# TensorE put into a written order in a two-block transformer kernel, with the first weights of a stage taken four at a time, weight splits held back at the norms and the attention heads handled in pairs

## The chip, the cores and the metric

One core of one Trainium2 chip runs the kernel. The metric is the device time of one execution in microseconds (us); the kernel before took 1275.31 us, the median of 3 runs (1269.11 to 1276.87 us).

## What is computed

256 positions of width 1024 go through two blocks of two layers each, in fp32. Cut to the lines that matter, the first block is

```python
for i in range(DEPTH):                      # 2
    hn = rmsnorm(h, norm_mix[i])
    mix = diff_attention(hn, ...) if i % 2 == 0 else neighborhood_attention(hn, ...)
    h = h + mix
    h = h + swiglu(rmsnorm(h, norm_ffn[i]), ffn_w_gate[i], ffn_w_up[i], ffn_w_down[i])
    gate = jax.nn.sigmoid(rmsnorm(h, norm_ple[i]) @ ple_w_gate[i])
    h = h + gate * (p[i] @ ple_w_proj[i])
```

and the second block is

```python
for layer in range(DEPTH):
    hn = rmsnorm_2(h, mix_norm_g[layer])
    h = h + (even_mixer(hn, ...) if layer % 2 == 0 else odd_mixer(hn, ...))
    h = h + conv_ffn(rmsnorm_2(h, ffn_norm_g[layer]), ...)
return rmsnorm_2(h, final_norm_g)
```

The differential attention ("da") has 8 heads with two 64-wide maps each, the neighbourhood attention ("na") 16 heads of 64, the odd mixer ("od") 8 forgetting and 8 T5-biased causal heads of 64. The hidden width of each of the four FFNs is 2816.

## The kernel before, in words

Activations lie with features on the 128 partitions and the 256 positions along the free axis. An fp32 product is made of three fp32r matmuls of a high and a low part (`mm3`, L207): hi·hi, hi·lo, lo·hi. One output tile of a 1024-deep product is 8 x 3 = 24 matmuls, a `pair` of output tiles (L329) 48.

Weights (L51 to L103) come in chunks of 128 x 1024: SyncE loads a chunk into one of 5 stage buffers, ScalarE writes its high part `w_hi` (L88), VectorE the low part `w_lo` (L89), into one of 8 pairs of buffers. `take` (L97) hands out the next finished chunk, and each call first splits the chunk that is six ahead.

Each stage ends in a norm. While the last down projections of a stage run bank by bank (`Acc.last`, L355), VectorE adds a bank to the residual `h`, and ScalarE and VectorE write the next stage's input `u_hi`, `u_lo` and its squares. `rstd_a` (L278) sums the squares on TensorE (`ps_ss`), VectorE scales (L287), GpSimd raises to the power -1/2 (L288); `rstd_b` spreads the result over the partitions by two transposes on TensorE (`ps_r`, L304) and a ScalarE copy `R` (L306). The products of the next stage start before `R` is there, since it is multiplied in after them.

Work that hangs on earlier results is put off with `at(delay, f)` (L214) and done by `tick()` (L218), which is called after every 12 matmuls. `rstd_soon` (L312) puts `rstd_a` one tick and `rstd_b` three ticks after the end of a stage. In attention the table LAG (L34) holds the delays of scores, transposes, values. One differential head lists 12 score matmuls (3 for each of two maps and two query halves). The other two kinds list the scores head by head: 6 fp32r matmuls for an na head; for an od head one fp32 product 128 wide and 3 fp32r matmuls. The two heads of a pair use partitions 0 to 63 and 64 to 127 of the same tiles.

The order on all engines is chosen by the scheduler of the language. It starts from the order in which the code is written, and may move an instruction past others on its engine.

The lines of the steps: FFN L733 (`silu_times` L722), gate ("ple") L779, even mixer ("ev") with its list of eight pairs L909, `small_constants` with 8 bias tiles of the differential attention on VectorE L507 to L511, `pair_steps` L588, the end `finish` L940.

Of the kernel before, what the change touches and what calls it, by code (L numbers as in the profile page):

```python
# [33 lines left out]
LAG = {"da": (2, 8, 11, 14), "da_every": 3, "pair": (2, 5, 7), "every": 2}  # L34
# [18 lines left out]
class Weights:  # L53
# [4 lines left out]
    def __init__(self, nc, stage, split, chunks):  # L58
        self.nc, self.stage, self.pool, self.chunks = nc, stage, split, chunks
        self.loaded, self.done, self.taken = [], [], 0  # L60
        self.n_load = self.n_split = 0

# [44 lines left out]
def network(ctx: ExitStack, tc: tile.TileContext, x_t, p_t, cols, b_v, na_bias, t5_bias, w_mats, out):  # L107
    nc = tc.nc

# [28 lines left out]
    def add_ffn(gu, down):  # L138
        for j in range(FT):
            add(gu, 2 * j, 2 * j + 1)  # L140
            if j >= 2 and j % 2 == 0:
                if j < FT - 2:
                    add(down, j - 2, j - 1)
        add(down, FT - 4, FT - 3, FT - 2, FT - 1)
# [167 lines left out]
    def rstd_soon(n, a=1, b=3):  # L312
# [16 lines left out]
    def pair(u, tag="g", bufs=2):  # L329
        ps = psum.tile([128, 2, S], F32, tag=tag, bufs=bufs, name="ps_g")  # L330
        for i in range(2):
            out_tile(ps[:, i, :], u)
        return ps

    class Acc:
# [19 lines left out]
        def last(self, xs, k0, done):  # L355
            ws = [W.take(1024) for _ in xs]
# [22 lines left out]
    def transposes(a, skip):  # L379

        w = 384 if skip else 512
        ps = psum.tile([128, 512], F32, tag=att_tag["T"][0], bufs=att_tag["T"][1], name="ps_t")
# [40 lines left out]
    def qkv_group(n, g, kind, bv, steps):  # L423
# [12 lines left out]
        ps = pair(u)  # L436
# [9 lines left out]
        ps = pair(u)  # L446
# [47 lines left out]
    def score(o, q, k, r, p, qt, w):  # L494
        c = slice(qt * 128, (qt + 1) * 128)
        if w < S:
            mm(o, q[0][r, p, c], k[0][r, p, :w], True, True)
        else:
            mm3(o, (q[1][r, p, c], q[2][r, p, c]), (k[1][r, p, :], k[2][r, p, :]), True, True)
# [31 lines left out]
    def da_steps(g, q, k, v, bias, o, emitted):  # L531
        for p in range(2):
# [3 lines left out]
            def scores(p=p, hd=hd, box=box):  # L536
                ps = [att_psum("S").rearrange("p (a b) -> p a b", a=2) for _ in range(2)]
                for qt in range(2):
                    for m in range(2):
                        score(ps[m][:, qt, :], q, k, slice(64 * m, 64 * m + 64), p, qt, S)  # L540
# [42 lines left out]

            for delay, f in zip(LAG["da"], (scores, trans, values, back)):
                at(LAG["da_every"] * p + delay, f)


    def pair_steps(g, q, k, v, bias_of, is_causal, o, emitted, later):  # L588
        for p in range(2):
            box = {}  # L590
            for e in range(2):
                hd = 4 * g + 2 * p + e
                r = slice(64 * e, 64 * e + 64)

                def scores(p=p, e=e, hd=hd, r=r, box=box):
                    widths = (128, 256) if is_causal else (256, 256)
                    bias = bias_of(hd)
                    ps = att_psum("S").rearrange("p (a b) -> p a b", a=2)
                    for qt in range(2):
                        score(ps[:, qt, :widths[qt]], q, k, r, p, qt, widths[qt])  # L600
                    sc = work.tile([128, 2, S], F32, tag="sc", bufs=3, name="sc")
                    st = softmax_pair(sc, ps, bias, widths)
# [5 lines left out]
                def trans(e=e, box=box):  # L608
                    box["t", e] = transposes(box["s", e], is_causal)

                every = LAG["every"]
                at(later + every * (2 * p + e) + LAG["pair"][0], scores)
                at(later + every * (2 * p + e) + LAG["pair"][1], trans)
# [13 lines left out]
            at(later + every * (2 * p + 1) + LAG["pair"][2], values)  # L627

    def attention(n, kind, gain_next):
# [4 lines left out]
        for g in range(4):  # L634
            bv = None
            if kind == "na":
# [3 lines left out]
                bias_of = lambda hd, bt=bt: (bt[:, hd % 4, 0, :], bt[:, hd % 4, 1, :])  # L640
            elif kind == "od" and g < 2:
                bias_of = lambda hd: fox_bias(hd, extra)
            elif kind == "od":
                bias_of = lambda hd: (t5_tiles[0][:, hd - 8, 128:], t5_tiles[0][:, hd - 8, :])
# [3 lines left out]
            def steps(q, k, v, g=g):  # L648
                if kind == "da":
                    da_steps(g, q, k, v, da_tiles, o, emitted)  # L650
                else:
                    pair_steps(g, q, k, v, bias_of, kind == "od", o, emitted, 5 if kind == "od" and g == 0 else 0)
# [38 lines left out]
    def fox_prepare(z, extra):  # L691
# [18 lines left out]
        cum()  # L710

    def fox_bias(hd, extra):
        ps = att_psum("V")
        for t in range(2):
            nc.tensor.transpose(ps[:, t * 128:(t + 1) * 128], extra["f"][:, t, hd:hd + 1].to_broadcast([128, 128]), ident)
        b = work.tile([128, 384], F32, tag="fb", bufs=2, name="fb")
        for qt, (a, w) in enumerate(((0, 128), (128, 256))):
            nc.vector.scalar_tensor_tensor(b[:, a:a + w], causal[:, S - w:], extra["f"][:, qt, hd:hd + 1],
                                           ps[:, :w], op0=OP.add, op1=OP.subtract)
        return b[:, :128], b[:, 128:]  # L720
# [12 lines left out]
    def ffn(n, middle, gain_next, finish=None):  # L733
        acc = Acc(FT)
        mids = {}
        for j in range(FT):
# [7 lines left out]
        for j in range(FT - 4, FT - N_LAST):  # L744
            acc.step(mids.pop(j), j)
# [33 lines left out]
    def ple(n, l, gain_next, after, final=False):  # L779
        nn = Norm()  # L780
        pt = [t.rearrange("p (k s) -> p k s", k=2) for t in p_split[l]]
        for b in range(4):
            hi, lo = W.take(512)
            pp = psum.tile([128, 2, S], F32, tag="m", bufs=2, name="ps_p")
# [4 lines left out]
            pg = pair(n.u)  # L789
            z = work.tile([128, 2, S], F32, tag="a", bufs=3, name="z")  # L790
            nc.vector.tensor_mul(z, pg, bc2(n.R))
            t = work.tile([128, 2, S], F32, tag="sc", bufs=3, name="tz")
            nc.scalar.activation(t, z, AF.Tanh, scale=0.5)
            nc.vector.scalar_tensor_tensor(t, t, 1.0, pp, op0=OP.add, op1=OP.mult)
            hb = h[:, 2 * b:2 * b + 2, :]
            nc.vector.scalar_tensor_tensor(hb, t, 0.5, hb, op0=OP.mult, op1=OP.add)
            norm_bank(nn, b, hb, gain_next)
            stats_bank(nn, b, hb)
            if final:
                stats_bank(nn, b, hb, True)  # L800
# [109 lines left out]
    for i, (f, a) in enumerate(plan):  # L910
        ps = pair(n.u, tags[i], 2 if tags[i] == "g" else 1)
# [27 lines left out]

    def finish():  # L940
# [3 lines left out]
        def done(b, ps):  # L944
# [4 lines left out]
            if b % 2 == 0:  # L949
                po.append([psum.tile([128, 512], F32, tag="g", bufs=2, name="po") for _ in range(2)] if b == 0 else  # L950
                          [psum.tile([128, 512], F32, tag=f"acc{t}", name="po") for t in range(2)])
            for i in range(2):
                k = 2 * b + i
                for t in range(2):
# [150 lines left out]
```

## Time and profile before

| what | value |
|---|---|
| median of 3 runs | 1275.31 us |
| the profiled execution | 1277.65 us, span 1275.8 us |
| PE (TensorE) busy | 1253.6 us, 98% |
| DVE (VectorE) busy | 932.6 us, 73% |
| ACT (ScalarE) busy | 697.3 us, 55% |
| POOL (GpSimd) busy | 31.6 us, 2% |
| mean granted TensorE clock | 0.996 |

The span is what the trace covers; 1.85 us of the execution lie around it. Busy time of PE is modelled, and matmuls overlap each other there, so what one matmul costs is read from the distance of its start to the next one's start, here called its slot. The stages lie in the span like this: loads to about 7 us, da attention to 134, FFN to 318, ple to 355, na attention to 476, FFN to 662, ple to 695, ev to 778, conv FFN to 953, od attention to 1080, conv FFN to 1266.

### The profile page before, as it was taken

What the parts mean: (1) busy time and instruction counts of PE and PEld (TensorE: products, weight loads), DVE (VectorE), ACT (ScalarE), POOL (GpSimd) and SP (SyncE); (2) the same over time, 40 slices, a digit from 0 to 9 for tenths busy, and PEclk for the clock granted to TensorE, in tenths of its full rate; (3) what the DMA queues carried; (4) which work ended last, traced back from release to release, by engine and by line L of the source; (5) the groups of instructions that cost most, each with busy time, mean ns of one, the idle gap of its engine ahead of it and who ended that gap; (6) DMA issues with size and microseconds to landing.
All of it is one profiled execution on the core that took longest, in us unless ns stands there. A gap on an engine that the chain in (4) does not pass through costs nothing.

```text
span 1275.8 us, 25715 instructions
## 1 busy us (share of the span) xinstructions
PE 1253.6 (98%) x10448; PEld 1223.2 (96%) x10448; DVE 932.6 (73%) x1708; ACT 697.3 (55%) x1178; POOL 31.6 (2%) x56
## 2 busy tenths in 40 slices
PE   6999999999999999999999999999999999999997
PEld 6999999999989999999999999999999899999997
DVE  7886866666976667666678888777787766877774
ACT  6776644444666654444457456455456565544543
POOL 1011000000010000000000000000000000000000
PEclk9999999999999999999999999999999999999999
DMA  8465555554646536555546375555545333655530
GB/s 292 150 195 184 167 184 194 192 184 150 212 152 186 175 116 199 187 197 186 176 141 207 132 247 183 183 185 196 182 153 197 102 132 131 209 188 183 188 127 34
DMA packets 62935, 222.46 MB, mean 174 GB/s; under 512 B 7264, under 2 KB 7776, under 8 KB 62688
## 3 DMA queue, kind: packets, MB, share of 16 engines
q1 hardware_dynamic: 60768, 214.52, 49.8%
q0 software_dynamic: 1616, 5.77, 1.9%
q8 instruction: 82, 1.34, 0.4%
q10 hardware_dynamic: 432, 0.53, 0.1%
q14 instruction: 37, 0.30, 0.1%
HBM read 219.74 MB, written 1.05 MB: 173 GB/s over the span
## 4 chain that ended last, share of the span: by engine, by line
PE 88%; DVE 4%; issue 3%; ACT 2%; POOL 1%; DMA 1%; POOLq 0%; DVEq 0%; ACTq 0%; SPq 0%
PE ps_g L202 50%; PE acc L202 25%; PE ps_v L202 5%; PE ps_S L202 3%; PE ps_V L202 2%; DVE w_lo L89 2%; PE ps_t L388 1%; ACT w_hi L88 1%; POOL rstd L288 1%; ACT u_hi L263 1%; PE ps_p L202 1%; PE pz L202 0%; PE ps_ss L202 0%; DVE u_lo L265 0%; DVE h L366 0%
## 5 line engine op out<-in xcount | busy, mean ns | idle before, releaser
L88 ACT ACTIVATE w_hi<-stage 128x1024 fp32r<-128x1024 f32 (+2 forms) x413 | 428.6, 1040 | 431.7 <-PE ps_g L202 170.0
L89 DVE TENSOR_TENSOR w_lo<-stage,w_hi 128x1024 fp32r<-128x1024 f32 (+2 forms) x413 | 495.3, 1201 | 212.1 <-ACT w_hi L88 209.0
L202 PE MATMUL ps_g<-u_hi,w_hi 128*128 128x256 f32 x2048 | 577.2, 283 | 7.9 <-ACT w_hi L88 7.2
L202 PE MATMUL ps_g<-u_hi,w_lo 128*128 128x256 f32 x2048 | 573.0, 280 | 1.0 <-DVE w_lo L89 1.0
L202 PE MATMUL ps_g<-u_lo,w_hi 128*128 128x256 f32 x2048 | 573.2, 280 | 0.4 <-DVE u_lo L265 0.4
L202 PEld LDWEIGHTS ps_g<-u_hi,w_hi 128*128 128x128 f32 x2048 | 384.4, 188 | 12.3 <-ACT w_hi L88 7.3
L202 PEld LDWEIGHTS ps_g<-u_hi,w_lo 128*128 128x128 f32 x2048 | 385.2, 188 | 1.7 <-DVE w_lo L89 1.4
L202 PEld LDWEIGHTS ps_g<-u_lo,w_hi 128*128 128x128 f32 x2048 | 385.2, 188 | 1.3 <-DVE u_lo L265 0.6
L202 PE MATMUL acc<-m,w_hi 128*128 128x256 f32 x1408 | 251.3, 280 | 0.3 <-DVE m L731 0.3
L202 PEld LDWEIGHTS acc<-m,w_hi 128*128 128x128 f32 x1408 | 215.2, 187 | 0.8 <-DVE m L731 0.6
L202 PE MATMUL acc<-m,w_lo 128*128 128x256 f32 x704 | 196.5, 279 | 0.0
L202 PEld LDWEIGHTS acc<-m,w_lo 128*128 128x128 f32 x704 | 132.2, 188 | 0.0
L202 PE MATMUL acc<-u_hi,w_hi 128*128 128x256 f32 x256 | 72.6, 287 | 0.0
L202 PE MATMUL acc<-u_lo,w_hi 128*128 128x256 f32 x256 | 71.3, 280 | 0.3 <-DVE u_lo L580 0.3
L202 PE MATMUL acc<-u_hi,w_lo 128*128 128x256 f32 x256 | 71.2, 280 | 0.0
L418 ACT ACTIVATE sc<-sc,st 128x256 f32<-128x256 f32 (+1 forms) x96 | 46.1, 482 | 19.2 <-DVE st L416 19.2
L202 PE MATMUL ps_v<-w_hi,u_hi 128*128 128x256 f32 x176 | 51.3, 292 | 0.0
L202 PE MATMUL ps_v<-w_lo,u_hi 128*128 128x256 f32 x176 | 49.5, 281 | 0.0
L202 PE MATMUL ps_v<-w_hi,u_lo 128*128 128x256 f32 x176 | 49.4, 281 | 0.0
L202 PEld LDWEIGHTS acc<-u_hi,w_hi 128*128 128x128 f32 x256 | 47.8, 188 | 1.5 <-issue 0.6
L202 PEld LDWEIGHTS acc<-u_lo,w_hi 128*128 128x128 f32 x256 | 48.1, 188 | 0.5 <-DVE u_lo L580 0.5
L202 PEld LDWEIGHTS acc<-u_hi,w_lo 128*128 128x128 f32 x256 | 48.0, 188 | 0.0
(191 smaller groups left out, 1218.8 us busy)
## 6 DMA issues: line engine op xcount, KB each, us to landing
stage<-w_gu SPq DMA_DIRECT2D x88, 512.0 KB, 4.2
stage<-w_in SPq DMA_DIRECT2D x88, 512.0 KB, 4.3
stage<-w_down SPq DMA_DIRECT2D x44, 512.0 KB, 4.3
stage<-w_out SPq DMA_DIRECT2D x44, 512.0 KB, 4.3
stage<-w_na_qkv SPq DMA_DIRECT2D x24, 512.0 KB, 4.0
stage<-w_da_qkv SPq DMA_DIRECT2D x23, 512.0 KB, 4.3
stage<-w_od_in SPq DMA_DIRECT2D x22, 512.0 KB, 3.3
stage<-w_gate SPq DMA_DIRECT2D x16, 512.0 KB, 3.3
```

Source lines behind the costliest of these rows:

```text
L88: self.nc.scalar.activation(hi[:, s], t[:, s], AF.Copy)
L89: self.nc.vector.tensor_sub(lo[:, s], t[:, s], hi[:, s].bitcast(F32))
L202: nc.tensor.matmul(o, a, b, start=start, stop=stop, **kw)
L263: nc.scalar.activation(n.u[0][:, 2 * b + i, :], src[:, i, :], AF.Copy, scale=gain(2 * b + i))
L288: nc.gpsimd.tensor_tensor(n.rstd, st[:, 2:4], mhalf, op=OP.pow)
L388: nc.tensor.transpose(ps[:, o:o + 128], a[:, qt, kk * 128:(kk + 1) * 128], ident)
L418: nc.scalar.activation(sc[:, i, :widths[i]], sc[:, i, :widths[i]], AF.Exp, bias=st[:, 2 + i:3 + i], accum_out=st[:, 4 + i:5 + i])
```

## The change

TensorE alone gets the written order (`manual_schedule`); the other engines stay with the scheduler. The code is written so that its order can stand:

- `first_pairs`: the first two pairs (four output tiles) of each stage except da run chunks 0 to 5 of all four tiles (72 matmuls) and then chunks 6 and 7 (24 matmuls). The sum of squares comes after 84 matmuls and the spread two ticks after that (`rstd_soon` with 7 and 9).
- From `Acc.last` on until four ticks after the next `rstd_soon`, `take` splits nothing (`hold`); the splits owed are done one per tick afterwards (`pay`).
- FFN: the middle parts (silu or conv) come one pair later, down steps too; the first three middles come at once. ple: gate products of the first two pairs together.
- Scores of the two row halves alternate matmul by matmul (`scores_of_two`), na and od heads are handled in pairs: one block of 12 scores (na) or 8 (od) instead of two of 6 or 4. Their transposes stand together. New delays in the table `AT`.
- The 8 bias tiles go from VectorE to GpSimd.
- The transposes back at the end come one or two banks later.

```diff
+AT = {
+    "da": {"scores": (3, 9), "then": (6, 8, 12), "last": ((2, 5), (5, 7, 10)), 0: (6, 10)},
+    "na": {"scores": (3, 9), "then": (6, 8), "last": ((2, 5), (5, 7)), 0: (6, 10)},
+    "od": {"scores": (3, 9), "then": (6, 8), "last": ((2, 5), (5, 7)), 0: (12, 15), 1: (6, 9)},
+}
...
+    def pay(self):
+
+        if self.owed and not self.hold:
+            self.owed -= 1
+            self.split()
+
     def take(self, n):
-        self.split()
+        if self.hold and self.taken < len(self.done):
+            self.owed += 1
+        else:
+            self.split()
...
+    ctx.enter_context(tc.manual_schedule(engines={mybir.EngineType.PE}))
...
     def tick():
         clock[0] += 1
+        W.pay()
...
-    def rstd_soon(n, a=1, b=3):
+    def release():
+        W.hold = False
+
+    def rstd_soon(n, a=7, b=9):
+        at(4, release)
         at(a, lambda: rstd_a(n))
         at(b, lambda: rstd_b(n))
...
+    def first_pairs(u, tags=("g", "g"), between=None, late=2):
...
+        for ks in (range(KT - late), range(KT - late, KT)):
+            for i in range(4):
...
+                if len(ws) == i:
+                    ws.append(W.take(KT * 128))
+                hi, lo = ws[i]
+                for k in ks:
+                    s = slice(k * 128, (k + 1) * 128)
+                    mm3(ps[i // 2][:, i % 2, :], (hi[:, s], lo[:, s]), (u[0][:, k, :], u[1][:, k, :]),
+                        k == 0 and i % 2 == 0, k == KT - 1, skip=True)
...
         def last(self, xs, k0, done):
+            W.hold = True
             ws = [W.take(1024) for _ in xs]
...
+    def scores_of_two(ps, q, k, p, widths):
+
+
+        for qt in range(2):
+            c, w = slice(qt * 128, (qt + 1) * 128), widths[qt]
+            terms = ((0, 0),) if w < S else ((1, 1), (1, 2), (2, 1))
+            for i, (a, b) in enumerate(terms):
+                for e in range(2):
+                    r = slice(64 * e, 64 * e + 64)
+                    mm(ps[e][:, qt, :w], q[a][r, p, c], k[b][r, p, :w], i == 0, i == len(terms) - 1)
...
-            nc.vector.tensor_scalar(da_tiles[hd // 4][:, hd % 4], dist, -2.0 ** (-8.0 * (hd + 1) / 8), None, op0=OP.mult)
+            nc.gpsimd.tensor_scalar(da_tiles[hd // 4][:, hd % 4], dist, -2.0 ** (-8.0 * (hd + 1) / 8), None, op0=OP.mult)
...
+            first, then = when(kind, g)
+            if prepare:
+                at(first[p] - 2, before)
+            at(first[p] + then[0], trans)
+            at(first[p] + then[1], values)
+            at(first[p], scores)
...
         for j in range(FT):
-            ps = pair(n.u)
-            m = work.tile([128, 2, S], F32R, tag=("qh", "kh")[j % 2], name="m")
-            mids[j] = (m[:, 0, :], m[:, 1, :])
-            middle(j, ps, n.R, mids[j])
-            if j >= 2 and j % 2 == 0 and j < FT - 2:
+            if j == 0:
+                held = list(enumerate(first_pairs(n.u)))
+            elif j > 1:
+                held.append((j, pair(n.u, *(("m", 2) if j == 2 else ("g", 2)))))
+
+            if j >= 2:
+                for i, ps in held:
+                    m = work.tile([128, 2, S], F32R, tag=("qh", "kh")[i % 2], name="m")
+                    mids[i] = (m[:, 0, :], m[:, 1, :])
+                    middle(i, ps, n.R, mids[i])
+                held.clear()
+            if j >= 3 and j % 2 == 1:
+                acc.step(mids.pop(j - 3), j - 3)
                 acc.step(mids.pop(j - 2), j - 2)
-                acc.step(mids.pop(j - 1), j - 1)
...
```

Three places show how instructions move. The first is TensorE in the na attention, where a head's scores stand (`ps_S` is a head's score tile, `ps_v` and `ps_g` are products with weights). Before:

```order
L202 MATMUL ps_v_4931<-w_lo_4619,u_hi_4162 128x256
L202 MATMUL ps_S_4969<-k_hi_4927,q_hi_4837 128x256
L202 MATMUL ps_S_4969<-k_lo_4928,q_hi_4837 128x256
L202 MATMUL ps_S_4969<-k_hi_4927,q_lo_4838 128x256
L202 MATMUL ps_S_4969<-k_hi_4927,q_hi_4837 128x256
L202 MATMUL ps_S_4969<-k_lo_4928,q_hi_4837 128x256
L202 MATMUL ps_S_4969<-k_hi_4927,q_lo_4838 128x256
L202 MATMUL ps_v_4931<-w_hi_4665,u_hi_4162 128x256
```

In the changed kernel the same place, on TensorE, begins:

```order
L220 MATMUL ps_g_4692<-u_hi_4324,w_lo_4471 128x256
L220 MATMUL ps_S_4723<-k_hi_4615,q_hi_4607 128x256
L220 MATMUL ps_S_4724<-k_hi_4615,q_hi_4607 128x256
L220 MATMUL ps_S_4723<-k_lo_4616,q_hi_4607 128x256
L220 MATMUL ps_S_4724<-k_lo_4616,q_hi_4607 128x256
L220 MATMUL ps_S_4723<-k_hi_4615,q_lo_4608 128x256
L220 MATMUL ps_S_4724<-k_hi_4615,q_lo_4608 128x256
L220 MATMUL ps_S_4723<-k_hi_4615,q_hi_4607 128x256
```

Before, six scores of one head stood alone, and the other head's six came about 25 matmuls of weights later; now the twelve of both heads stand in one block, the two heads in turn.

The second is VectorE at the norm ahead of the first FFN (`half` is the folded sum of squares, `rstd` its scaling, `gu` the first step of a middle part). Before:

```order
L89 TENSOR_TENSOR w_lo_1851<-stage_1634,w_hi_1850 128x1024
L272 TENSOR_TENSOR half_1831<-ssq_1745 128x256
L89 TENSOR_TENSOR w_lo_1896<-stage_1683,w_hi_1895 128x1024
L287 TENSOR_SCALAR rstd_1835<-ps_ss_1830 128x2
L89 TENSOR_TENSOR w_lo_1926<-stage_1718,w_hi_1925 128x1024
L755 TENSOR_TENSOR gu_1886<-ps_g_1811,R_1871 128x512
L89 TENSOR_TENSOR w_lo_1966<-stage_1724,w_hi_1965 128x1024
```

In the changed kernel VectorE has there:

```order
L97 TENSOR_TENSOR w_lo_1906<-stage_1655,w_hi_1905 128x1024
L291 TENSOR_TENSOR half_1912<-ssq_1735 128x256
L306 TENSOR_SCALAR rstd_1916<-ps_ss_1911 128x2
L97 TENSOR_TENSOR w_lo_1932<-stage_1685,w_hi_1931 128x1024
L97 TENSOR_TENSOR w_lo_1939<-stage_1861,w_hi_1938 128x1024
L97 TENSOR_TENSOR w_lo_1957<-stage_1873,w_hi_1956 128x1024
L97 TENSOR_TENSOR w_lo_1980<-stage_1891,w_hi_1979 128x1024
L835 TENSOR_TENSOR gu_2010<-ps_g_1801,R_1965 128x512
L835 TENSOR_TENSOR gu_2019<-ps_g_1802,R_1965 128x512
```

The split between `half` and `rstd` is gone; four splits stand between `rstd` and the first middle part, where one stood.

The third is GpSimd's queue at the start, up to the first power -1/2 of a norm (`rstd`) and the first of the differential heads (`st2`). Before:

```order
L816 MEMSET ug1_197 128x2
L816 MEMSET ug2_198 128x2
L639 DMA bv_4459<-b_v 128x256
L288 TENSOR_TENSOR rstd_231<-rstd_231,mhalf_110 128x2
L568 TENSOR_TENSOR st2_642<-st2_642,mhalf_110 128x2
```

In the changed kernel GpSimd has:

```order
L911 MEMSET ug1_199 128x2
L911 MEMSET ug2_200 128x2
L705 DMA bv_4461<-b_v 128x256
L573 TENSOR_SCALAR bias_120<-dist_108 128x512 x4
L573 TENSOR_SCALAR bias_121<-dist_108 128x512 x4
L307 TENSOR_TENSOR rstd_324<-rstd_324,mhalf_112 128x2
L628 TENSOR_TENSOR st2_692<-st2_692,mhalf_112 128x2
```

The eight bias tiles now stand ahead of the first norm's power on GpSimd; they read `dist`, which VectorE finishes.

## Rows read from the trace of the kernel before

**Rows 1.** The chain that ended last: by engine, then by line.

```profile
PE 88%; DVE 4%; issue 3%; ACT 2%; POOL 1%; DMA 1%; POOLq 0%; DVEq 0%; ACTq 0%; SPq 0%
```

**Rows 2.** Waits of PE: for what, us in total, times, longest us.

```profile
PE ps_r L304 <- POOL rstd L288: 3.7, 5, 2.6
PE ps_r L304 <- DVE rstd L295: 1.3, 1, 1.3
...
PE ps_ss L202 <- DVE half L272: 0.4, 1, 0.4
...
PE ps_g L202 <- ACT u_hi L263: 0.2, 1, 0.2
```

**Rows 3.** PE on score tiles in da, na, od: window, its us, PE busy (count), clock.

```profile
30.00:130.00 100.00, 9.63 (x96) 1.00 0.56 175
360.00:460.00 100.00, 15.99 (x96) 1.00 0.54 168
970.00:1065.00 95.00, 13.95 (x80) 1.00 0.38 131
```

**Rows 4.** PE timeline at one da head's scores: start us, us, what.

```profile
81.40 0.39 PE L202 MATMUL ps_S<-k_hi,q_hi 64*128 64x256 f32 x2
...
82.09 0.30 PE L202 MATMUL ps_S<-k_hi,q_lo 64*128 64x256 f32 x2
82.31 0.38 PE L202 MATMUL ps_g<-u_hi,w_hi 128*128 128x256 f32 x1
```

**Rows 5.** PE timeline at one na head's scores.

```profile
389.76 0.28 PE L202 MATMUL ps_v<-w_lo,u_hi 128*128 128x256 f32 x1
389.96 0.38 PE L202 MATMUL ps_S<-k_hi,q_hi 64*128 64x256 f32 x1
...
390.87 0.39 PE L202 MATMUL ps_v<-w_hi,u_hi 128*128 128x256 f32 x1
```

**Rows 6.** PE timeline at one od head's scores.

```profile
1020.80 0.49 PE L202 MATMUL ps_S<-k,q 64*128 64x128 f32 x2
1021.05 0.36 PE L202 MATMUL ps_S<-k_hi,q_hi 64*128 64x256 f32 x1
...
1021.58 0.39 PE L202 MATMUL ps_v<-w_hi,u_hi 128*128 128x256 f32 x1
```

**Rows 7.** PE timeline at the first norm.

```profile
24.04 0.69 PE L304 MATMUL ps_r<-ident,rstd 128*128 128x128 f32 x2 [2.58 <-POOL rstd L288]
```

**Rows 8.** Engines just after it: PE, PEld, DVE, ACT, POOL busy (count), granted clock.

```profile
24.00:27.30 3.30, 3.26 (x16) 3.26 (x17) 1.87 (x3) 2.54 (x4) 0.00 (x0) 0.51 0.79 277
```

**Rows 9.** Timeline of POOL at the first norm.

```profile
20.63 3.36 POOL L288 TENSOR_TENSOR rstd<-rstd,mhalf 128x2 f32<-128x2 f32 x1 [17.82 <-DVE rstd L287]
```

**Rows 10.** Groups of POOL: shapes, count, busy us, mean ns, idle before.

```profile
L288 POOL TENSOR_TENSOR rstd<-rstd,mhalf 128x2 f32<-128x2 f32 x11 | 10.9, 993 | 1080.5 <-DVE rstd L287 1080.5
...
L181 POOL IOTA dist<- 128x512 f32 x1 | 0.6, 557 | 0.0
```

**Rows 11.** Timeline of DVE at the start: the first bias tile.

```profile
11.83 0.42 DVE L511 TENSOR_SCALAR bias<-dist 128x512 f32<-128x512 f32 x1
```

**Rows 12.** Timeline of DVE after the na scores of rows 5.

```profile
390.98 0.42 DVE L414 CUSTOM_DVE_ANT_0 sc<-ps_S,na_bias_t 128x256 f32<-128x256 f32 x1 [1.45 <-PE ps_S L202]
...
391.67 1.22 DVE L89 TENSOR_TENSOR w_lo<-stage,w_hi 128x1024 fp32r<-128x1024 f32 x1
...
394.86 0.61 DVE L604 TENSOR_SCALAR sc<-sc,st 128x256 f32<-128x256 f32 x2
```

**Rows 13.** Engines in na and in ev: PE, PEld, DVE, ACT, POOL busy (count), clock.

```profile
366.00:447.00 81.00, 81.00 (x631) 72.68 (x631) 55.91 (x155) 50.20 (x107) 7.23 (x12) 1.00 0.56 173
709.00:745.00 36.00, 35.74 (x302) 35.35 (x301) 35.03 (x84) 18.30 (x28) 0.00 (x0) 1.00 0.47 159
```

**Rows 14.** Engines in two stretches of FFNs, columns as in rows 13.

```profile
200.00:212.00 12.00, 12.00 (x104) 12.00 (x103) 7.74 (x11) 6.18 (x9) 0.00 (x0) 1.00 0.65 207
875.00:887.00 12.00, 12.00 (x108) 12.00 (x108) 8.93 (x14) 6.41 (x10) 0.00 (x0) 1.00 0.58 203
```

More of the change, by code (lines that the diff above doesn't have):

```diff
@@ L332, in pair @@
             out_tile(ps[:, i, :], u)
+        return ps
+    def first_pairs(u, tags=("g", "g"), between=None, late=2):
+        ps = [psum.tile([128, 2, S], F32, tag=t, bufs=2 if t in "gm" else 1, name="ps_g") for t in tags]
+        ws = []
+        done = 0
+        for ks in (range(KT - late), range(KT - late, KT)):
+            for i in range(4):
+                if between and i % 2 == 0 and len(ws) < 4:
+                    between(i // 2)
+                if len(ws) == i:
[5 more added lines that the diff above has]
+                        k == 0 and i % 2 == 0, k == KT - 1, skip=True)
+                    done += 1
+                    if done % 4 == 0:
+                        tick()
         return ps
@@ L435, in qkv_group @@
         u = n.u
-        ps = pair(u)
+        ps_k = None
+        if g == 0 and kind != "da":
+            ps, ps_k = first_pairs(u)
+        else:
+            ps = pair(u)
+            if g == 0:
+                ps_k = pair(u)
+        while g == 0 and not hasattr(n, "R"):
+            tick()
         if kind == "na":
@@ L492, in qkv_group, with when @@
                 nc.scalar.activation(v[:, t, :], pv[:, t, :], AF.Copy, scale=n.rstd[:, t:t + 1])
[L494 to L499, printed above, removed]
+    def scores_of_two(ps, q, k, p, widths):
[6 more added lines that the diff above has]
+                    mm(ps[e][:, qt, :w], q[a][r, p, c], k[b][r, p, :w], i == 0, i == len(terms) - 1)
+    def when(kind, g):
+        t = AT[kind]
+        return t["last"] if g == 3 else (t.get(g, t["scores"]), t["then"])
     lam = const.tile([128, 4], F32, name="lam")
@@ L582, in back, with pair_steps, before, scores @@
                 emitted.add(hd)
-            for delay, f in zip(LAG["da"], (scores, trans, values, back)):
-                at(LAG["da_every"] * p + delay, f)
-    def pair_steps(g, q, k, v, bias_of, is_causal, o, emitted, later):
+            first, then = when("da", g)
+            for delay, f in zip((0,) + then, (scores, trans, values, back)):
+                at(first[p] + delay, f)
+    def pair_steps(g, q, k, v, kind, bias_of, prepare, o, emitted):
+        is_causal = kind == "od"
+        widths = (128, 256) if is_causal else (256, 256)
         for p in range(2):
             box = {}
[L591 to L600, printed above, removed]
+            def before(p=p, box=box):
+                box["bias"] = bias_of(4 * g + 2 * p)
+            def scores(p=p, box=box, before=before):
+                if "bias" not in box:
+                    before()
+                ps = [att_psum("S").rearrange("p (a b) -> p a b", a=2) for _ in range(2)]
+                scores_of_two(ps, q, k, p, widths)
+                for e in range(2):
                     sc = work.tile([128, 2, S], F32, tag="sc", bufs=3, name="sc")
-                    st = softmax_pair(sc, ps, bias, widths)
+                    st = softmax_pair(sc, ps[e], box["bias"][e], widths)
                     for qt in range(2):
@@ L606, in scores, with trans @@
                     box["s", e] = sc
[L608 to L613, printed above, removed]
+            def trans(box=box):
+                for e in range(2):
+                    box["t", e] = transposes(box["s", e], is_causal, "TV"[e])
             def values(p=p, box=box):
@@ L651, in steps @@
                 else:
[L652 removed]
+                    pair_steps(g, q, k, v, kind, bias_of, kind == "od" and g < 2, o, emitted)
             qkv_group(n, g, kind, bv, steps)
@@ L910, in network @@
     for i, (f, a) in enumerate(plan):
-        ps = pair(n.u, tags[i], 2 if tags[i] == "g" else 1)
+        if i == 0:
+            first = first_pairs(n.u, tags[:2])
+        ps = first[i] if i < 2 else pair(n.u, tags[i], 2 if tags[i] == "g" else 1)
         waiting.append((f, ps, a))
```

112 lines of the change are left out of this document (66 added, 46 removed).

## Prediction

> **What bounds the kernel now.** I read the chain that ended last first: 88% of the span is TensorE's own work and no other engine has more than 4% [rows 1]. A change can then win in two ways only: TensorE's work gets shorter, or its waits go. The waits come next. After the initial loads TensorE waits 3.7 us in five places for GpSimd's power of a norm, of which one is 2.6 us, 1.3 us once for the second statistics of the even mixer, and 0.2 to 0.4 us each in six more places, 1.9 us together (the first and the last of the six stand there) [rows 2]. So outside the start 1.1 + 1.3 + 1.9 = 4.3 us of waits are all there is to take, in a span of 1276 us. The third view is TensorE's work on the score tiles: 96 matmuls are 9.63 us of busy time in da, the same 96 are 15.99 us in na, and 80 are 13.95 us in od [rows 3]. That gap is the largest thing the change touches.
>
> **Scores.** The timeline says where the gap comes from. A da head lists its two maps together, on the two halves of the partitions; matmuls of one kind start in twos (x2), and twelve are through from 81.40 to 82.31, 0.91 us [rows 4]. An na head lists six, all on one half, and they take 0.91 us as well, from 389.96 to 390.87, after 0.20 us that pass between the last weight product's start and the first score [rows 5]. So twelve on both halves cost what six on one cost: one block is 1.11 us either way. The change puts the two heads of a pair into one block.
> - na: 16 blocks become 8, 8 x 1.11 = 8.9 us less. If the halves did not run side by side, only the switching would be saved: six more slots at 12.00 / 104 = 0.115 us [rows 14] are 0.69, a block of 1.80 against 2.22, 8 x 0.42 = 3.4 us less.
> - od: a head is 0.78 us from 1020.80 to 1021.58 [rows 6], plus the same 0.20: 0.98. One block for two saves 8 x 0.98 = 7.8 us if all goes side by side. The trace shows no fp32 products on both halves at once; if they run one after the other, 1021.05 - 1020.80 = 0.25 comes back per block and 5.8 us are saved; with nothing side by side (0.25 and three slots) 8 x (0.98 - 0.60) = 3.0. I take 6.8, between the first two, since the fp32r terms are those of rows 4.
> - da: a whole block is busy from 81.40 to 82.09 + 0.30, 0.99 us [rows 4]; eight would be 7.9, and rows 3 have 9.63, so some blocks were torn by the scheduler. In the fixed order they are whole: 1.5 us less (0 to 1.7).
>
> Together -17.2 us, and -6.4 at the least.
>
> **Norms.** Splits are kept off VectorE between `half` and `rstd`, and 72 products of the new stage stand ahead of the last bank. In the FFNs and ple 24 matmuls (2.8 us) stand between `ps_ss` and `ps_r`, as before, but without the split of 1.22 us [rows 12] in VectorE's queue; the waits there should go. At na and od code spins the ticks on, so 12 matmuls, 1.4 us, stand between; a power of (10.9 - 3.36) / 10 = 0.75 us [rows 9, 10] with two hand-overs to other engines is longer than the rest of that, and the wait of today remains. In ev the two statistics come in one sum but the second power still hangs on the first: the 1.3 us remain. Of the 4.3 us I take 2.3 as gone; the bounds are 4.3 and, if the waits only move, 0. What comes next: four splits, 4 x 1.22 = 4.9 us, now stand ahead of the first middle part, and its 0.7 us free a PSUM buffer that the fourth pair needs. From `rstd` on that is some 6 us, an estimate from these rows; TensorE has 12 + 48 matmuls, 6.9 us, till then. It just fits: 0, or up to 1.2 us lost at each of four FFNs if one split more is in the way.
>
> **Start.** At the first norm `ps_r` waits 2.58 us [rows 7] for a power that takes 3.36 us from 20.63 on [rows 9]; then 16 matmuls take 3.30 us at a granted clock of 0.51 [rows 8], the 1.2 GHz level, where the same 16 slots are 1.8 us at full clock. At stake: 2.6 + 1.5 = 4.1 us. The change puts eight bias tiles ahead of this power. They can start where VectorE started its first, 11.83 [rows 11]. GpSimd's one 128x512 row, an iota, takes 0.56 us [rows 10]: done by 16.3, no harm. Its longest row is 3.36: done at 38.7, some 18 us late. I take the iota's side, the same shape on the same engine, where even 1.1 us each ends by 20.6. Nine more matmuls ahead of `ps_r` (96 instead of 87) cover 1.0 us. If the first power again takes 3.36, 1.0 us is gained; if it takes the usual 0.75 since GpSimd's first arithmetic went to a tile, all 4.1. I take 2.0.
>
> The two ends have a rule beside them. The first power's 3.36 us against 0.75 of the others is 2.6 us of something that is paid once [rows 9, 10]. The Trainium skill (GPSIMD Engine Reference, 2.1 Instruction dispatch) says that the first call to a freshly loaded kernel pays about 6 us to load its code; the trace has less than half of that at the first power. By that rule, if each operation is loaded by itself, the power pays again behind the tiles, which pay too, and the term is 1.0 us at best; if the cost belongs to the first arithmetic of any kind, it is 4.1.
>
> **What the fixed order costs.** An order that TensorE must follow turns lateness elsewhere into waits. In na VectorE starts on a head's scores at 390.98 and has them scaled at 394.86 + 0.61 = 395.47, 4.5 us with one split between [rows 12]. The change gives 72 matmuls, 8.3 us, but now for two heads; the second one's share of VectorE is about 2 us (two reads and two scalings at 0.3 to 0.4 each, and small ones), 6.5 in all. One split more fits, two don't. VectorE is busy 55.91 of 81.00 us in na, and 35.03 of 36.00 in ev [rows 13], where nothing can be gained. For 24 blocks and the transposes and values behind them I add 3 us, between 0 and the 24 x 1.2 of the rival below.
>
> **Sum.** -17.2 - 2.3 - 2.0 + 3.0 = -18.5. The profiled execution took 1277.65 us (span 1275.8 and 1.85 around it), 2.3 above the median of 1275.31, so -18.5 leaves 1259.1 for it and 1256.8 for the median: 1257.
>
> **Rivals.**
> - *Lateness in attention (slower).* At each of 24 blocks k_lo and q_lo are needed at a fixed place, and VectorE's queue is the scheduler's. From two splits more than now ahead of them, TensorE waits 1.2 us at each: +29 us. A wait of 2.58 us was followed by the low clock [rows 7, 8]; half of the blocks with that add 12 x 1.5 = 18. With what else is won: 1257 - 3 + 29 + 18 = 1301; without the clock, 1283. It decides from 0.9 us a block on. For it: 24 places, each with 6.5 of 8.3 us used. Against: 30% of VectorE's time in na is free.
> - *The halves don't run side by side* as the two heads are different tiles: -6.4 instead of -17.2, 1268, no change that counts. Against it stands the x2 of rows 4.
> - *GpSimd is slow on the tiles.* At 2.2 us each they end at 29.4, the first power is 9 us late, and the start loses 9 + 2.6 instead of gaining 2: 1268.
> - *Another pace.* The same matmuls run 104 in 12 us in one stretch and 108 in another, at full clock [rows 14]. If the fixed order puts two more FFNs (about 360 us) on the quicker pace, that is 360 x 4 / 104 = 14 us less: 1243. The order doesn't touch the steady part of an FFN, so I can't say which.
> - *The order is what the scheduler had.* Then nothing moves; the listings of the change show otherwise.
>
> **How the numbers follow.** Forecast 0.60, quicker pace 0.08, attention late 0.11, halves serial 0.09, slow tiles 0.08, anything else 0.04. About 1% (12.8 us) can be told from no change here. Faster by over 1%, below 1262.6: most of the first two, 0.65. Within 1%: serial halves, slow tiles and the forecast's upper part, 0.24. Slower by over 1%: 0.11. The low end, 1242, is the quicker pace or all gains in full with no new waits (-18.4 - 4.3 - 4.1 = -26.8, 1249) and some pace; the high end, 1272, takes in the two cases at 1268 and a few waits; the late attention is left out.
>
> **What would show it.** TensorE's busy time on score tiles in na near 8 us and near 8 in od; waits of `ps_r` for GpSimd gone in FFN and ple, still there at na, od and ev; the first power starting by 21 us; no waits for `k_lo`, `sc` or `at`. Wrong: score blocks of 1.8 us, waits of over 0.5 us in most of the attention's groups, or a start that loses time.

## The result, and the profile after

The changed kernel took 1255.20 us, the median of 4 runs (1249.32 to 1255.85), beside 1275.94 us for the kernel before (4 runs, 1269.11 to 1276.87). The ratio is 0.9858 with a 95% interval of 0.9826 to 0.9891: 1.4% faster by the ratio, where 1257 was forecast. Its profiled execution took 1255.70 us, span 1253.9 us, 21.9 less than before. The total came out as forecast, but not by the forecast terms alone: the start lost time instead of gaining it, and a change of TensorE's pace, which the sum had left out, made up for it. The views are taken in the order of the prediction.

The chain that ended last, by engine, which answers to [rows 1]:

```profile
PE 86%; DVE 6%; issue 3%; POOL 2%; ACT 2%; DMA 1%; POOLq 0%; DVEq 0%; ACTq 0%; SPq 0%
```

TensorE's share fell by two points and VectorE's and GpSimd's rose: more of the path is now waiting. The waits of TensorE (for what, us in total, times, longest), beside [rows 2]:

```profile
PE ps_r L323 <- POOL rstd L307: 9.0, 4, 7.6
...
PE ps_g L220 <- ACT u_hi L282: 2.5, 2, 1.9
PE ps_S L220 <- ACT k_hi L475: 1.3, 1, 1.3
PE ps_r L323 <- DVE rstd L314: 1.2, 1, 1.2
...
PE ps_S L220 <- DVE k_lo L476: 0.6, 2, 0.3
```

The small waits at the FFN and ple norms are gone, as forecast. But the wait at the first norm grew from 2.6 to 7.6 us, 2.5 us stand where ple hands over to the next stage, and the attention waits for `k_hi` and `k_lo` now and then. All in all TensorE waits 25 us by the whole list, 10 more than before.

TensorE's busy time on score tiles in da, na and od (window, its length, busy time and count, clock), beside [rows 3]:

```profile
30.00:130.00 100.00, 8.08 (x96) 0.95 0.54 169
360.00:460.00 100.00, 8.09 (x96) 1.00 0.58 188
950.00:1050.00 100.00, 7.31 (x80) 1.00 0.45 156
```

9.63, 15.99 and 13.95 us became 8.08, 8.09 and 7.31. One block of na in the timeline of TensorE (start, us, what), beside [rows 4, 5]:

```profile
374.20 0.28 PE L220 MATMUL ps_g<-u_hi,w_lo 128*128 128x256 f32 x1
374.41 0.39 PE L220 MATMUL ps_S<-k_hi,q_hi 64*128 64x256 f32 x2
...
375.32 0.39 PE L220 MATMUL ps_g<-u_hi,w_hi 128*128 128x256 f32 x1
```

Twelve matmuls take 0.91 us, in twos (x2), and the whole block 1.12 us: what six took before.

The start went the other way. GpSimd's timeline, its group of tiles (count, busy us, mean ns), and TensorE's spread behind it, beside [rows 7, 9]:

```profile
11.73 18.50 POOL L573 TENSOR_SCALAR bias<-dist 128x512 f32<-128x512 f32 x8 [8.93 <-DVE dist L571]
30.20 0.73 POOL L307 TENSOR_TENSOR rstd<-rstd,mhalf 128x2 f32<-128x2 f32 x1
```

```profile
L573 POOL TENSOR_SCALAR bias<-dist 128x512 f32<-128x512 f32 x8 | 18.2, 2290 | 9.2 <-DVE dist L571 8.9
```

```profile
30.98 0.69 PE L323 MATMUL ps_r<-ident,rstd 128*128 128x128 f32 x2 [7.57 <-POOL rstd L307]
```

The tiles held the queue until 30.2 us, and the power behind them, 0.73 us long, came 9.6 us later than before. The last view is the pace. Windows just after that wait and in the four FFNs (PE, PEld, DVE, ACT, POOL busy with counts, granted clock), beside [rows 8, 14]:

```profile
30.90:35.20 4.30, 4.22 (x20) 4.22 (x21) 2.83 (x3) 3.50 (x6) 0.02 (x1) 0.50 0.01 2
200.00:212.00 12.00, 12.00 (x108) 12.00 (x107) 8.27 (x12) 6.48 (x9) 0.00 (x0) 1.00 0.55 173
560.00:572.00 12.00, 12.00 (x108) 12.00 (x107) 8.29 (x12) 6.33 (x9) 0.00 (x0) 1.00 0.56 188
875.00:887.00 12.00, 12.00 (x104) 12.00 (x103) 8.76 (x15) 5.85 (x9) 0.00 (x0) 1.00 0.53 178
1150.00:1162.00 12.00, 12.00 (x104) 12.00 (x103) 8.29 (x13) 5.34 (x7) 0.00 (x0) 1.00 0.54 187
```

The clock was at its lower level after the long wait, as before. It was there again behind the waits at the second ple's end (1.9 and 0.6 us; granted clock 0.57 from 677 to 681 us) and behind the wait for `k_hi` in da (0.58 from 104 to 108 us). The first two FFNs run 108 matmuls in 12 us, 4 more than the stretch from 200 us of [rows 14] (the second row there is from a quick stretch of 17 us in the third FFN, which is gone). By the distances of starts they keep this pace from 151 to 331 and from 478 to 658 us, so 2 x 180 x 4/104 = 13.8 us were gained in stretches whose code the change hardly touches. Score tiles (-16.1), waits (+10) and this pace add up to some -20 us of the 21.9; the other 2 are not assigned. That became the main question of the experiments.

### The profile page after: what moved, and what is told of

Same layout as the page of the kernel before. It is cut to its first block, busy times and chain, and to the rows that moved or that the text cites. A ratio compares the mean times of both kernels' runs of the same rounds, so it can differ in the third digit from the quotient of the medians.

```text
span 1253.9 us, 25715 instructions
## 1 busy us (share of the span) xinstructions
PE 1219.8 (97%) x10448; PEld 1199.9 (96%) x10448; DVE 930.2 (74%) x1700; ACT 693.4 (55%) x1178; POOL 56.5 (5%) x64
## 4 chain that ended last, share of the span: by engine, by line
PE 86%; DVE 6%; issue 3%; POOL 2%; ACT 2%; DMA 1%; POOLq 0%; DVEq 0%; ACTq 0%; SPq 0%
PE ps_g L220 50%; PE acc L220 26%; PE ps_v L220 4%; DVE w_lo L97 2%; PE ps_V L220 2%; POOL bias L573 1%; PE ps_S L220 1%; PE ps_t L433 1%; POOL rstd L307 1%; ACT w_hi L96 1%; PE ps_p L220 1%; ACT sc L463 0%; PE pz L220 0%; DMA stage<-w_ev_out 0%; PE ps_ss L220 0%
## 5 line engine op out<-in xcount | busy, mean ns | idle before, releaser
L220 PE MATMUL acc<-m,w_hi 128*128 128x256 f32 x1408 | 246.5, 278 | 0.1
L307 POOL TENSOR_TENSOR rstd<-rstd,mhalf 128x2 f32<-128x2 f32 x11 | 15.7, 1426 | 1036.6 <-DVE rstd L306 1036.6
```

The source lines that it names most:

```text
L220: nc.tensor.matmul(o, a, b, start=start, stop=stop, **kw)
L307: nc.gpsimd.tensor_tensor(n.rstd, st[:, 2:4], mhalf, op=OP.pow)
```

## The experiments

Times are medians, each with the ratio to the kernel before run on the same chip. e1 and e3 to e5 ran on one chip, e6 to e9 on a second, e10 and e12 on a third, where the kernel before took 1276.29, 1273.26 and 1275.73 us; so a difference in us between runs of two chips is good to about 3 us, and what the traces show is put beside it. Two theories stood at the beginning: GpSimd's tiles cost the start, and the score blocks win because both halves of the array work side by side. Rivals were the fixed order, the held splits, and later the pace.

**e1: bias tiles back on VectorE.**

```diff
-            nc.gpsimd.tensor_scalar(da_tiles[hd // 4][:, hd % 4], dist, ...)
+            nc.vector.tensor_scalar(da_tiles[hd // 4][:, hd % 4], dist, ...)
```

> The changed kernel with its eight bias tiles back on VectorE. Theory (GpSimd is held up while VectorE runs splits, and the tiles in front of the first power cost the start): VectorE has spare time there, a tile is 0.4 us on it, the first power starts near 21.5 us and takes 1.5 to 3.4 us beside splits; the wait of ps_r falls from 7.57 us to 0.5 to 2.5, the stretch at the low clock gets short; total 6 to 9 us less than the changed kernel, 1246 to 1249 us. Rival (the start is hidden, later stages wait for weights anyway): no change, 1255. Rival (the first power always pays for loading its code): the power takes 3.36 us even with nothing beside it.

1247.38 us (1246.01 to 1248.16), ratio 0.9769 (0.9752 to 0.9785): 7.8 us less than the changed kernel (8.1 by the spans of the two traces, 1253.9 and 1245.8). The power at the start, from GpSimd's timeline, and the spread, from TensorE's:

```profile
22.14 2.56 POOL L307 TENSOR_TENSOR rstd<-rstd,mhalf 128x2 f32<-128x2 f32 x1 [19.33 <-DVE rstd L306]
```

```profile
24.76 0.69 PE L323 MATMUL ps_r<-ident,rstd 128*128 128x128 f32 x2 [2.32 <-POOL rstd L307]
```

The start is on the path, and the move of the tiles cost 7.8 us. The first power is not long by itself: behind the tiles, with VectorE idle, it took 0.73 us; here, with a split and three of the tiles on VectorE at the same time, 2.56.

**e3: scores of a block head by head.**

```diff
-            for i, (a, b) in enumerate(terms):
-                for e in range(2):
-                    r = slice(64 * e, 64 * e + 64)
+            for e in range(2):
+                r = slice(64 * e, 64 * e + 64)
+                for i, (a, b) in enumerate(terms):
```

> The changed kernel with the scores of a block listed head by head (three of one head, three of the other, and so on) instead of in turn. Theory (the two halves of the array run side by side as soon as both heads' matmuls stand in one block, as in the differential heads before): 96 scores of the neighbourhood attention stay near 8.1 us of busy time, time as the changed kernel, 1250 to 1256. Rival (only listing in turn lets them overlap): 12 to 16 us for these 96 and as much more in the other two attentions, total 1262 to 1275.

1255.84 us (1255.49 to 1256.33), ratio 0.9837 (0.9823 to 0.9852): no change from the changed kernel. The na scores, in the view of [rows 3]:

```profile
360.00:460.00 100.00, 8.25 (x96) 1.00 0.58 184
```

Listing in turn is not needed. That both heads stand in one block is what counts.

**e4: the scheduler orders TensorE, from the new code.**

```diff
-    ctx.enter_context(tc.manual_schedule(engines={mybir.EngineType.PE}))
```

> The changed kernel without the written order: the scheduler orders TensorE again, from the new code. Theory (the gain comes from the score blocks and from what stands ahead of the norms in the code): most score blocks stay whole, some are torn as before, norms lose some tenths of a us each, total 1256 to 1264. Rival (the fixed order itself makes the gain): back near the kernel before, 1268 to 1276. Rival (fixed order only costs): 1245 to 1252, with the waits at the ple ends and the da attention gone.

1249.99 us (1243.68 to 1250.26), ratio 0.9779 (0.9755 to 0.9804). Without the written order the kernel is 5.2 us faster. The waits behind ple show one reason:

```profile
PE ps_g L219 <- ACT u_hi L281: 1.0, 2, 0.7
```

They are 1.0 us instead of 2.5, and the second power's wait in ev falls from 1.2 to 0.2 us. By the whole lists TensorE waits 20.4 us instead of 25.5, 5.1 less, which is the difference in time. The third form of the expectation held by its time, the fixed order only costs, but not in all its places: the da attention's wait for `k_hi` is still 1.3 us. The gain is in how the code is written.

**e5: splits wait for the power (a measuring kernel).** The high part of a split that follows a norm's sum is scaled by a 1.0 worked out from the power. The hold on splits is also let go later, at the sum of squares.

```diff
+                    self.nc.scalar.activation(hi[:, s], t[:, s], AF.Copy, scale=self.gate)
...
+        nc.vector.tensor_scalar(one, n.rstd[:, 0:1], 0.0, 1.0, op0=OP.mult, op1=OP.add)
+        W.gate = one
```

> A measuring kernel: the splits that follow a norm's sum of squares wait for its power (their high part is scaled by a 1.0 that is computed from the power), so VectorE has no split to run while GpSimd does the power. Theory (a power that starts inside a split ends only after it): powers of the norms take 0.7 us instead of 1.55 to 1.64; the waits of ps_r at the na, ev and od norms (0.52, 0.52, 0.42 us) go to 0.1 or less; the FFNs get new waits, since six splits in a row come ahead of the first middle part. Total 1255 to 1270. Rival (powers got slow for another reason, as GpSimd switching between two kinds of operation): they stay at 1.5 us and more.

1304.46 us in a single run, 34 above the expected range. By its list TensorE waits 50 us instead of 25, some 13 of them for `w_hi` and `w_lo` after the first load; the rest was not taken apart. The expected waits of 0.1 us or less came at ev and od, but na's `ps_r` waited 1.7 us. What the run was made to measure is clear. GpSimd's powers in the changed kernel and, second, here (count, busy us, mean ns):

```profile
L307 POOL TENSOR_TENSOR rstd<-rstd,mhalf 128x2 f32<-128x2 f32 x11 | 15.7, 1426 | 1036.6 <-DVE rstd L306 1036.6
```

```profile
L311 POOL TENSOR_TENSOR rstd<-rstd,mhalf 128x2 f32<-128x2 f32 x11 | 7.6, 695 | 1095.2 <-DVE rstd L310 1095.2
```

The mean halves as soon as no split runs beside them, so the rival, another reason than the splits, is out. One of them in detail, ahead of the first FFN in the changed kernel, GpSimd and then VectorE:

```profile
147.31 1.61 POOL L307 TENSOR_TENSOR rstd<-rstd,mhalf 128x2 f32<-128x2 f32 x1 [19.52 <-DVE rstd L306]
```

```profile
147.15 3.50 DVE L97 TENSOR_TENSOR w_lo<-stage,w_hi 128x1024 fp32r<-128x1024 f32 x3
```

The power starts 0.16 us into the first of three splits that follow one another, 1.2 us each, and ends at 148.92, half a us after the first and inside the second.

**e6: the spread one tick earlier (on e1), so that it waits.**

```diff
-    def rstd_soon(n, a=7, b=9):
+    def rstd_soon(n, a=7, b=8):
```

> The kernel of e1 (bias tiles on VectorE) with the spread of the FFN and ple norms one tick earlier, so that 12 matmuls and not 24 stand between sum of squares and spread. Direct price: ps_r waits 0.4 to 0.6 us at the four FFN norms, 2 us in all. Theory (a spread that doesn't wait sends TensorE into the quicker pace of 113 ns a matmul, one that waits leaves it at 118): the first two FFNs run at 118, 6.5 to 7 us each more: 1262 to 1264 against 1247 for e1. Rival (the pace has nothing to do with the norm's wait): 1248 to 1250, first two FFNs still at 113.

1266.57 us over 10 runs (1253.53 to 1268.70), ratio 0.9946 (0.9916 to 0.9976): 19.2 us more than e1. The first two FFNs, in e1 and then here:

```profile
200.00:212.00 12.00, 12.00 (x108) 12.00 (x107) 8.21 (x11) 6.24 (x9) 0.00 (x0) 1.00 0.71 222
560.00:572.00 12.00, 12.00 (x108) 12.00 (x108) 7.95 (x10) 4.85 (x6) 0.00 (x0) 1.00 0.60 204
```

```profile
200.00:212.00 12.00, 12.00 (x104) 12.00 (x104) 7.81 (x11) 6.49 (x9) 0.00 (x0) 1.00 0.67 204
560.00:572.00 12.00, 12.00 (x104) 12.00 (x103) 7.10 (x10) 5.29 (x7) 0.00 (x0) 1.00 0.54 179
```

And the spread ahead of the second FFN with matmuls behind it, in e1 and then here:

```profile
469.85 0.38 PE L323 MATMUL ps_r<-ident,rstd 128*128 128x128 f32 x2
...
470.41 0.28 PE L220 MATMUL ps_g<-u_hi,w_hi 128*128 128x256 f32 x1
...
470.97 0.28 PE L220 MATMUL ps_g<-u_hi,w_lo 128*128 128x256 f32 x1
```

```profile
475.06 0.43 PE L323 MATMUL ps_r<-ident,rstd 128*128 128x128 f32 x2 [0.45 <-POOL rstd L307]
...
475.45 0.28 PE L220 MATMUL ps_g<-u_lo,w_hi 128*128 128x256 f32 x1
...
475.92 0.28 PE L220 MATMUL ps_g<-u_hi,w_lo 128*128 128x256 f32 x1
```

In e1 five matmuls from 470.41 on take 0.56 us, 0.112 each, here four from 475.45 on take 0.47, 0.118 each; ahead of the spread both run at 0.118. So the pace changes at the spread itself, or stays. Waits of `ps_r` grew by 1.4 us for GpSimd and, in ev, by 2.9 us for the second power (4.1 instead of 1.2); others shrank, and by the whole lists TensorE waits 23.0 us against 20.4, 2.6 more. The pace of both FFNs fell back and took 13.8 us with it, which with the waits is 16.4 of the 18.8 us between the two spans (1264.6 and 1245.8). A wait of some 0.4 us at each of these two norms went with 7 us more in the FFN behind it.

Two things on record limit this. At the fourth FFN of the same trace the spread waits 0.42 us as well, and the quick pace follows, for 11 us. And one of the ten executions took 1253.53 us, 10 less than any other; it has no trace. The edit also moves the spread 12 matmuls forward; in the kernel before it stands after 24, as in e1, and the pace behind it was 118 there, so the place alone doesn't decide.

**e7: e1 and e4 together.**

```diff
-    ctx.enter_context(tc.manual_schedule(engines={mybir.EngineType.PE}))
...
+            nc.vector.tensor_scalar(da_tiles[hd // 4][:, hd % 4], dist, ...)
```

> e1 and e4 together: bias tiles on VectorE, TensorE ordered by the scheduler from the new code. Theory (both add, since they are at different places): 1250 - 8 = 1242, faster than both kernels. Rival (the scheduler tears something at the start once VectorE has the tiles): 1246 to 1252.

1242.42 us (1240.62 to 1243.22), ratio 0.9767 (0.9729 to 0.9806): by the medians the two add up, as expected. The ratio doesn't show it (0.9769 in e1), as the kernel before took from 1267.64 to 1276.41 us on this chip; the traces do, with spans of 1245.8 and 1240.0 us and 20.4 and 15.1 us of TensorE's waits in e1 and here.

**e8: no split held back (on e1).**

```diff
-            W.hold = True
```

> e1 without holding back splits at the norms (each take splits at once, as in the kernel before). Theory (splits ahead of the norm delay the last bank and the folded sum, so ss or the spread waits again): ps_ss or ps_g wait 0.3 to 1 us at most norms, powers somewhat shorter than 1.6 where no split runs beside them; if a spread waits in the first two FFNs their pace is lost too: 1252 to 1265. Rival (72 matmuls ahead of the last bank cover the splits by themselves, the hold only bunches them): 1245 to 1249.

1247.12 us (1240.46 to 1249.78), ratio 0.9798 (0.9751 to 0.9845), as e1's 1247.38. The rival held: the hold brings nothing here, and TensorE's waits are 21.0 us by the list, against 20.4 in e1. The powers did not get shorter either (1593 ns in the mean, 1594 in e1). That it is the 72 matmuls ahead of the last bank that cover the splits was not tested by itself. Its profiled execution, at 1240.46, had the third FFN at the quick pace as well, which the other three runs, to judge by their times, had not.

**e9: the two heads of a pair one tick apart in na and od (on e1).**

```diff
-                scores_of_two(ps, q, k, p, widths)
+                one_head(0, p, box, ps)
+                at(1, lambda: one_head(1, p, box, ps))
```

> e1 with the two heads of a pair apart in the na and od attention: the second head's scores come one tick, 12 matmuls, after the first head's. Theory (a block of six on one half costs what twelve on both cost): TensorE's busy time on 96 na scores back to 16 us, on 80 od scores to near 14; 8 x 1.1 + 8 x 0.8 to 1.0 = 15 to 17 us more than e1, 1262 to 1264. Rival (matmuls of the other head are kept from overlapping by something else, the gain was elsewhere): 1247 to 1251.

1261.11 us (1250.41 to 1262.31), ratio 0.9897 (0.9842 to 0.9953): 13.7 us more than e1. Score tiles of na and od:

```profile
355.00:455.00 100.00, 15.85 (x96) 1.00 0.55 168
950.00:1050.00 100.00, 13.44 (x80) 1.00 0.44 145
```

They are back where they were before the change [rows 3], 13.9 us more than in e1 (8.09 and 7.30). So the pairing alone is worth some 14 us in these two stages, a little less than the 15 to 17 expected. One of the four executions took 1250.41 us; it has no trace.

**e10: down steps of the conv FFNs one pair later (on e7).** In e7 the third FFN came out of its norm at the quick pace and lost it at its first down step, where two matmuls took from 759.50 to 760.07, 0.57 us instead of 0.23 (TensorE's timeline). The edit is set for the two conv FFNs alone (`late`), and loads their weights in the new order:

```profile
759.39 0.28 PE L219 MATMUL ps_g<-u_hi,w_lo 128*128 128x256 f32 x1
759.50 0.73 PE L219 MATMUL acc<-m,w_hi 128*128 128x256 f32 x2
760.07 0.28 PE L219 MATMUL acc<-m,w_lo 128*128 128x256 f32 x1
```

```diff
+            if late and j >= 4 and j % 2 == 0:
+                acc.step(mids.pop(j - 4), j - 4)
+                acc.step(mids.pop(j - 3), j - 3)
             if j >= 2:
                 for i, ps in held:
...
-            if j >= 3 and j % 2 == 1:
+            if not late and j >= 3 and j % 2 == 1:
```

> The kernel of e7 with the down steps of the two conv FFNs one pair of tiles later (before the middle part of pair j = 4, 6, ...), since the first down step of a conv FFN waits some 0.2 us for its middle part, and the quicker pace ended there in e7 (759.5 us). Theory (a wait of TensorE is where the pace is drawn anew): that wait is gone; the third FFN stays at 113 ns a matmul wherever it came out of its norm at that pace, 6 to 7 us less: 1234 to 1237. Rival (the conv FFNs fall to the slow pace for another reason): 1241 to 1244.

1236.19 us (1234.56 to 1241.37), ratio 0.9697 (0.9676 to 0.9718), the fastest version. The third FFN in e7 and then here:

```profile
765.00:905.00 140.00, 140.00 (x1191) 140.00 (x1190) 105.59 (x166) 71.11 (x100) 0.00 (x0) 1.00 0.57 190
```

```profile
765.00:905.00 140.00, 140.00 (x1237) 140.00 (x1237) 110.41 (x176) 74.88 (x105) 0.00 (x0) 1.00 0.61 197
```

46 more matmuls fit into 140 us, which is 5.2 us in this stretch, and 6.2 us were gained in all. One of the four executions took 1241.37 us, the time of e7.

**e12: e10 without the hold.** The edit is that of e8.

> e10 without holding back splits at the norms. Theory (the hold does nothing here, as e8 against e1 showed): the time of e10 within 2 us. Rival (with the hold gone the last bank or the sum waits, and the pace of an FFN goes): 4 to 14 us more than e10.

1236.30 us (1235.30 to 1241.95, five runs), ratio 0.9699 (0.9678 to 0.9721): the same as e10, one execution at 1241.95 included.

## Why the prediction was right, and where its steps were not

*Scores* (-17.2 forecast): right in mechanism and size. By busy time -7.9 in na, -6.6 in od and -1.6 in da, 16.1 together; e9 puts 13.7 of it on the pairing in na and od. The rival of halves that don't run side by side is out, by the x2 in the timeline and by e3. The na term was 1 us too large: the 1.11 us of a block take in the slot of the weight product ahead of it, 0.118 us, which stays, and 8 x (1.11 - 0.118) = 7.9 is what was measured. In od the fp32 products of two heads do run side by side, in seven of eight blocks: the same subtraction from the forecast's 0.98 us a head gives 6.9, and 6.6 were measured.

*Norms* (-2.3): the waits at the FFN and ple norms went, as said. But those of the other norms did not stay, they grew: na's from 0.2 to 0.5 us, od's from nothing to 0.4, and ev's first power now waits 0.5 besides the 1.2 of the second, since powers take 1.6 us instead of the 0.75 of the forecast. Outside the start `ps_r` waits 2.6 us, 2.4 before: the 2.3 did not come. And the step priced only the waits. What it left out is the pace behind a norm, and that is the larger part.

*Start* (-2.0): wrong in sign. "I take the iota's side, the same shape on the same engine" is the step that failed: a tile reads `dist` and took 1.5 us alone where the iota, which reads nothing, took 0.56, and the forecast had no term for VectorE's splits beside it. Among the tiles with nothing on VectorE beside them the shortest took 1.49 us; another took 7.02 beside splits (count, minimum, median, maximum in ns):

```profile
L573 POOL TENSOR_SCALAR bias<-dist x8: 1489/1568/7019, 11.7 to 28.7; 128x512 f32<-128x512 f32 x8
```

The mean of 2.29 us is the case of the rival of slow tiles (2.2 us each), which was given 0.08 and put at 11.6 us lost; e1 measures 7.8 against the same kernel with the tiles on VectorE.

*The one-off cost of GpSimd's first power.* The 3.36 us of [rows 9] were read as something paid once, with the Trainium skill's first call (GPSIMD Engine Reference, 2.1 Instruction dispatch) beside it. No run here shows a first call that is longer: the first power took 0.73 us in the changed kernel, and starts as the tiles end. The 3.36 us, from 20.63 to 23.99, were a power that shared its time with VectorE's work, in the kernel before (VectorE's timeline):

```profile
20.39 0.41 DVE L511 TENSOR_SCALAR bias<-dist 128x512 f32<-128x512 f32 x1
20.72 1.21 DVE L89 TENSOR_TENSOR w_lo<-stage,w_hi 128x1024 fp32r<-128x1024 f32 x1
21.86 0.41 DVE L511 TENSOR_SCALAR bias<-dist 128x512 f32<-128x512 f32 x1
22.19 1.21 DVE L89 TENSOR_TENSOR w_lo<-stage,w_hi 128x1024 fp32r<-128x1024 f32 x1
```

The Trainium skill's GPSIMD Engine Reference also says (2. Architecture) that GpSimd's read and write port is shared with VectorE. The trace agrees as far as it goes, with 0.70 us for powers alone and 1.6 beside splits; that it is the port, and nothing else the two share, no run here shows.

*What the fixed order costs* (+3.0): right in direction. Comparing e4 with the changed kernel gives 5.2 us, e7 with e1 5.0. The places were others than forecast, too: not transposes and values in na, but the hand-over from ple (2.5 us, 1.0 in e4, and 0.6, gone there) and the second power in ev (1.2, and 0.2 in e4). One wait for `k_hi` in da (1.3) is new, too, but e4 has it as well, so it is not the fixed order's. The rival of late scores at 24 blocks did not come; three blocks waited.

*Pace*: the rival that was given 0.08 and priced at 14 us is what happened, 13.8 us. "The order doesn't touch the steady part of an FFN" was the wrong reason to set it aside: in the first two FFNs the pace of the steady part is set at the norm in front of it. In nine kernels with new code and no wait of `ps_r` at the norms of the first two FFNs (one trace each), all 18 of these FFNs ran at 113 ns a matmul. In the kernel before and in e6, where `ps_r` waits, all four ran at 118; the second FFN of the kernel before, its spread and its pace:

```profile
483.88 0.43 PE L304 MATMUL ps_r<-ident,rstd 128*128 128x128 f32 x2 [0.23 <-POOL rstd L288]
```

```profile
560.00:572.00 12.00, 12.00 (x104) 12.00 (x103) 7.47 (x10) 4.85 (x6) 0.00 (x0) 1.00 0.56 184
```

At its first FFN the wait is too short for the list: the spread starts 0.23 us behind the matmul ahead of it instead of 0.12. e5 is the exception: `ps_r` waits at neither norm, the first FFN ran at 113 and the second at 118, where the spread fell into a stretch at the lower clock (granted 0.57 from 490 to 494 us). So the wait at the norm is the best single sign in these traces, and e6 the only test of it.

So the sum of -18.5 had the scores right, missed the start by 10 us, the norms and the fixed order by some 2 us each on one side and the pace by 14 us on the other, and the errors nearly cancelled. The range held, but a good part of the hit is luck.

What stays open: the third FFN came out of a norm without a wait at the quick pace in six of nine kernels, the fourth in one of nine, and there for 10 us only. The kernel before and e6 had the fourth FFN at the quick pace at first, behind a spread that was held up. In e8 the third FFN kept the pace across the very same late first down step at which e7 lost it. So a wait does not always end the pace, and no wait does not always bring it; what decides at the level of single matmuls was not found.

## What to carry to other kernels

Where TensorE is busy 98% of the time, look at the distance between its matmuls before looking at its waits: two stretches of equal work at 104 and 108 matmuls in 12 us are a bigger lever than all the waits together, and in two of the four FFNs here a wait of under half a us at the stage's start went with the slower one. Products of 64 rows belong in one block with the products of the other 64 rows, whatever the order inside the block. Don't put work on GpSimd ahead of something that TensorE waits for while VectorE runs long instructions from SBUF to SBUF.

## What the runs showed of the hardware

- GpSimd is held up while VectorE runs splits: the power of 128 x 2 took 0.70 us alone and 1.55 to 1.64 beside splits, a 128 x 512 tile 1.49 alone and up to 7.02.
- TensorE runs the same 256-column fp32r products at two steady distances, 113 and 118 ns, at the full granted clock, for up to 180 us at a time, and was seen to change between them where the stream was interrupted or delayed, though not at every such place.
- Matmuls on the two 64-row halves start within 0.02 us of each other even where the program lists three of one half and then three of the other (8.25 us for 96 na scores in e3, 8.09 in turn).
